# Encoder block on one core: eight instead of five of eleven down pairs by seven products, weight sums made ahead and kept in memory, one ring for weights, MLP chunks by pairs

## The chip, the cores and the metric

The kernel runs on one core of one Trainium2 chip. The metric is the device time of one execution in microseconds (us). Before the change, three runs gave 1457.05 to 1457.96 us, median 1457.39. The engines are named as in the profile: PE (matrix products), PEld (its loads of the stationary operand), DVE (vector engine), ACT (scalar engine), POOL, and SP, whose queue starts the loads.

## The reference, cut to what matters

```
x: (256, 2048) f32; D_FF = 5632
h = rms_norm(x); proj = h @ w_in                      # (2048, 10240)
ya = windowed_gqa(...); yb = dilated_attention(...)
x = x + (sigmoid(ga) * (ya @ w_branch_a) + sigmoid(gb) * (yb @ w_branch_b)) @ w_out
hf = rms_norm(x)
g = depthwise_conv3(hf @ w_ffn_gate) + conv_b
x = x + (gelu(g) * (hf @ w_ffn_up)) @ w_ffn_down      # the MLP: the change is mostly here
x = x + sigmoid(rms_norm(x) @ w_ple_gate) * (p @ w_ple_proj)
return rms_norm(x)
```

All data is f32. The gelu is computed by its tanh form.

## The kernel before, in words

**Precision.** A weight w is used as two parts: hi, which ACT rounds from w (L264), and lo = w - hi, which DVE makes (L265). Activations have two parts too. A product is hi times hi, plus the two cross terms. Where activations are the moving operand (`unit_blocks`, stages A and E) one block of 128 weight columns takes a matmul of 512 columns (L308) and one of 256 (L315). Where weights move (`thirds`, L365 to L367, stages B, D, F, pp, G) a product of 128 tokens, 128 inputs and 512 outputs takes three matmuls of 512 columns.

**Weights.** The host lays all weights out as pieces of 1 MB (128 x 2048 f32) in the order of use. SP loads one piece at a time into a ring of three buffers (`raw`). `produce` converts it by units of 1024 or 512 columns. The results go to rings of six units (`uh`, `ul`) and, for sums of weights, two more (`vh`, `vl`). A unit is converted as soon as `drop` has freed a place, so ACT and DVE run ahead of PE by at most the rings.

**Stages.** A: input projection and attention. B0 to B3: the gates, with the branch projections. D0, D1: output projection. Then the MLP in two halves of 22 chunks of 128 of the 5632 features: E0 makes the activations of a half (gate and up products of each chunk, 16 blocks each, then the convolution, gelu and product in `mlp`), F00 and F01 multiply them by the down weights, each for 1024 of 2048 output columns; then E1, F10, F11. pp and G end the block: projection of p, gate, final norm.

**Seven products for eight.** A stage of quads goes through its weights in pieces of two input chunks (a pair, 256 inputs) by two groups of 512 columns: four quarters. With two token halves, a plain piece (`s`) takes 8 products, 24 matmuls. A piece marked `S` takes 7 products (a Strassen-like scheme): four use sums of quarters of the weights and sums of the activations (`sums_of`). It has seven quarters to convert (3.5 units of 1024 columns) where a plain piece has four (two units), and DVE makes the weight sums in place (L257 to L259) in the stage itself. The table for the down stages is `DOWN = "SsSsSsSsSss"`: five of eleven pairs. `row_sums` puts the seven results together at the end of a stage.

**MLP chunks.** `mlp` handles one chunk of gate or up at a time, on tiles of 256 tokens: for gate, two reads of the product, the norm's factor, the convolution's three taps, then gelu; for up, factor, product with gelu, and the two parts for F (`halves`). The jobs go g0, g1, u0, g2, u1, ...

**End.** After the last stage each token half's last 512 columns are finished by columns of 256; then the sum of squares (L1109 to L1112), a power on POOL (L1114), the scaled rows (L1121) and the stores.

**Order.** PE, ACT, DVE and SP each have one queue in program order. The order on an engine is set when the kernel is built: by the program, within which a scheduler lets ready work go ahead of waiting work. Loads wait on the SP queue until their buffer is free.

## Time and profile before

| | |
|---|---|
| three runs | 1457.05, 1457.39, 1457.96 us |
| the profiled execution | 1457.96 us, of which the span is 1456.2 us |
| mean granted TensorE clock | 0.998 |
| PE, DVE, ACT busy | 99%, 86%, 56% of the span |
| read from and written to HBM | 279.49 and 2.14 MB |
| E0 | about 638.7 to 875 us of the span |
| F00, F01 | 875 to 988 |
| E1 | 988 to 1233 |
| F10, F11 | 1233 to 1349 |

"Busy" is time in which an instruction of the engine was under way. Matmuls overlap: each is recorded with its whole duration, and the next begins before it ends. So the time that one costs is the distance between starts. The same holds, to a lesser degree, for DVE and ACT.

### The profile page before, as it was taken

The numbers are of one execution on the slowest core, as the hardware profiler recorded it, in microseconds if no ns is written. First come the engines' busy times: TensorE is split into PE (matmuls) and PEld (weight loads), VectorE is DVE, ScalarE is ACT, GpSimd is POOL, SyncE is SP. The second block draws the span as 40 slices with busy tenths as digits, with TensorE's granted clock in tenths as the row PEclk, the third lists the DMA queues.
The fourth block names the chain that finished last, engine by engine and source line by source line (L and its number), as shares of the span: only waits on it lengthen the run. The fifth ranks groups of instructions, "written<-read, shape, count | busy, mean of one in ns | idle before, by whom it ended". The sixth has DMA issues, their size and how long they took to land.

```text
span 1456.2 us, 19520 instructions
## 1 busy us (share of the span) xinstructions
PE 1444.5 (99%) x7488; PEld 1235.9 (85%) x7488; DVE 1248.8 (86%) x1849; ACT 822.1 (56%) x1141; POOL 4.1 (0%) x9
## 2 busy tenths in 40 slices
PE   9999999999999999999999999999999999999997
PEld 8888888888888888888888888888888888888785
DVE  7677665679998989989888899989888889999995
ACT  7455544446555656666555555455555555565762
POOL 0000000000000000000000000000000000000000
PEclk9999999999999999999999999999999999999999
DMA  9654444535546456465554545565555554546462
GB/s 335 249 206 146 152 168 175 175 141 203 192 187 235 180 213 234 174 232 193 186 199 175 202 152 221 176 254 183 199 184 193 185 192 173 193 191 234 170 237 81
DMA packets 46312, 282.88 MB, mean 194 GB/s; under 512 B 4932, under 2 KB 9668, under 8 KB 13964
## 3 DMA queue, kind: packets, MB, share of 16 engines
q1 hardware_dynamic: 45500, 280.46, 53.2%
q8 instruction: 58, 0.95, 0.3%
q10 hardware_dynamic: 720, 1.19, 0.2%
q14 instruction: 34, 0.28, 0.1%
HBM read 279.49 MB, written 2.14 MB: 193 GB/s over the span
## 4 chain that ended last, share of the span: by engine, by line
PE 97%; DVE 1%; ACT 1%; issue 1%; DMA 0%; SPq 0%; POOL 0%; POOLq 0%; DVEq 0%; ACTq 0%
PE bank L308 29%; PE bank L315 15%; PE bank L365 14%; PE bank L366 14%; PE bank L367 14%; PE bank L354 2%; PE bank L356 2%; PE bank L355 2%; PE bank L292 1%; PE bank L293 1%; PE bank L870 1%; PE bank L687 0%; PE bank L635 0%; PE bank L634 0%; PE bank L633 0%
## 5 line engine op out<-in xcount | busy, mean ns | idle before, releaser
L264 ACT ACTIVATE uh<-raw 128x1024 fp32r<-128x1024 f32 (+2 forms) x518 | 522.3, 1017 | 399.5 <-PE bank L308 183.6
L265 DVE TENSOR_TENSOR ul<-raw,uh 128x1024 fp32r<-128x1024 f32 (+2 forms) x518 | 596.8, 1169 | 128.9 <-ACT uh L264 68.8
L308 PE MATMUL bank<-hf,uh 128*128 128x512 f32 x1408 | 336.3, 391 | 0.0
L308 PEld LDWEIGHTS bank<-hf,uh 128*128 128x128 f32 x1408 | 258.9, 188 | 50.2
L315 PEld LDWEIGHTS bank<-hf,ul 128*128 128x128 f32 x1408 | 180.4, 191 | 6.7
L315 PE MATMUL bank<-hf,ul 128*128 128x256 f32 x1408 | 182.8, 283 | 0.0
L264 ACT ACTIVATE vh<-raw 128x1024 fp32r<-128x1024 f32 x92 | 97.4, 1058 | 57.0 <-DVE raw L257 25.4
L265 DVE TENSOR_TENSOR vl<-raw,vh 128x1024 fp32r<-128x1024 f32 x92 | 111.9, 1219 | 0.4
L308 PE MATMUL bank<-hs,uh 128*128 128x512 f32 x432 | 103.6, 392 | 0.0
L456 ACT ACTIVATE t<-bank 128x256 f32<-128x256 f32 x122 | 46.5, 384 | 96.6 <-PE bank L315 89.5
L308 PEld LDWEIGHTS bank<-hs,uh 128*128 128x128 f32 x432 | 79.5, 188 | 15.6
L365 PE MATMUL bank<-uh,act 128*128 128x512 f32 x232 | 90.4, 390 | 0.0
L366 PE MATMUL bank<-ul,act 128*128 128x512 f32 x232 | 90.4, 390 | 0.0
L367 PE MATMUL bank<-uh,act 128*128 128x512 f32 x232 | 90.3, 389 | 0.0
L365 PE MATMUL bank<-uh,hs 128*128 128x512 f32 x172 | 67.3, 391 | 0.0
L367 PE MATMUL bank<-uh,hs 128*128 128x512 f32 x172 | 67.3, 391 | 0.0
L366 PE MATMUL bank<-ul,hs 128*128 128x512 f32 x172 | 67.1, 390 | 0.0
L257 DVE TENSOR_TENSOR raw<-raw 128x1024 f32<-128x1024 f32 x46 | 56.1, 1221 | 0.6
L315 PE MATMUL bank<-hs,ul 128*128 128x256 f32 x432 | 56.6, 284 | 0.0
L315 PEld LDWEIGHTS bank<-hs,ul 128*128 128x128 f32 x432 | 54.5, 191 | 1.0
L366 PE MATMUL bank<-vl,S 128*128 128x512 f32 x138 | 54.1, 392 | 0.1
L365 PE MATMUL bank<-vh,S 128*128 128x512 f32 x138 | 54.1, 398 | 0.0
(240 smaller groups left out, 2273.2 us busy)
## 6 DMA issues: line engine op xcount, KB each, us to landing
raw<-in_wts SPq DMA_DIRECT2D x251, 1024.0 KB, 4.8
raw<-in_wts SPq DMA_DIRECT2D x12, 512.0 KB, 7.2
xr<-in_xrow SPq DMA_DIRECT2D x4, 512.0 KB, 8.3
x<-in_xt SPq DMA_DIRECT2D x13, 128.0 KB, 6.0
hb<-hold SPq DMA_DIRECT2D x3, 514.0 KB, 5.9
hb<-hold SPq DMA_DIRECT2D x2, 768.0 KB, 7.5
last<-in_gainrow SPq DMA_DIRECT2D x1, 1024.0 KB, 6.9
out<-xr SPq DMA_DIRECT2D x4, 256.0 KB, 2.6
```

Source lines behind the costliest of these rows:

```text
L257: nc.vector.tensor_tensor(raw[:, :2 * WIDE], raw[:, WIDE:3 * WIDE], raw[:, :2 * WIDE], op=ALU.subtract)
L264: nc.scalar.activation(hi, src, AF.Copy)
L265: nc.vector.tensor_tensor(lo, src, hi.bitcast(F32), op=ALU.subtract)
L308: nc.tensor.matmul(acc, weights(u)[0][:, o * P:(o + 1) * P], m, start=first, stop=False, skip_group_check=True)
L315: nc.tensor.matmul(acc[:, T:], weights(u)[1][:, o * P:(o + 1) * P], m[:, :T], start=False, stop=last, skip_group_check=True)
L354: nc.tensor.matmul(acc[:, :n * P], xh, hi, start=(k == 0), stop=False)
L355: nc.tensor.matmul(acc[:, :n * P], xh, lo, start=False, stop=False)
L356: nc.tensor.matmul(acc[:, :n * P], xl, hi, start=False, stop=(k == KC - 1))
L365: nc.tensor.matmul(acc, sh, wh, start=first, stop=False, skip_group_check=True)
L366: nc.tensor.matmul(acc, sh, wl, start=False, stop=False, skip_group_check=True)
L367: nc.tensor.matmul(acc, sl, wh, start=False, stop=last, skip_group_check=True)
L456: keep(nc.scalar.activation(t, acc[:, T:], AF.Copy, scale=scale))
```

## The change

It has six parts.

1. **More pieces by seven products.** The down table becomes `ZZsZSZsZSZs`: eight of eleven pairs by seven products in each of the four F stages.
2. **Sums kept in memory.** Six of the eight are of a new kind `Z`. During E0 and E1 both halves of such a piece are loaded once more, DVE makes its four sums in place (`keep_sums`), and SP stores them to a buffer in HBM (`store_sums`). `_SUMS_AT` puts twelve of these into each half, after the 6th piece of the half and after every third from there. In F, a `Z` piece loads two quarters from the weights and four sums from that buffer, and needs no DVE sums. Every `S` piece, in the other stages too, now makes its sums into two tiles of their own, with four operations on 512 columns (L302 to L305) in place of one on 1024 and two on 512.
3. **One ring.** Raw weights and low parts share a ring of 12 tiles of 128 x 1024 (`SPLIT`); high parts have a ring of 7 (`ROUND`). Loads are of a unit (512 KB or 256 KB) and run at least four ahead of the conversion (`AHEAD`). The loads of the start are asked for step by step (`EARLY`).
4. **Pairs of chunks.** `mlp` reads each product at once but does the rest for two chunks together on tiles of 2 x 256; the middle tap moves to ACT, and a constant of the gelu into ACT's scale. An up chunk comes two gate chunks behind (`LAG`).
5. **The last products.** The last six matmuls of 512 columns are no longer cut into twelve of 256.
6. **The end.** On DVE the sum's last step (L1206) is kept ahead of the product with the gains (L1209).

PE's matmuls: 7452 - 6 = 7446 in place of 7488: 36 fewer in F, six fewer at the end.

```
-DOWN = "SsSsSsSsSss"
+DOWN = "ZZsZSZsZSZs"
...
     jobs = []
-    for f in range(FHALF + 1):
+    for f in range(FHALF + LAG):
         if f < FHALF:
             jobs.append(("g", half * FHALF + f))
-        if f:
-            jobs.append(("u", half * FHALF + f - 1))
+        if f >= LAG:
+            jobs.append(("u", half * FHALF + f - LAG))
...
+    for half in range(2):
+        ahead("E%d" % half, ("F%d0" % half, "F%d1" % half), 5, 3)
...
-        elif kind == "S":
-            cuts = [("n", 0, WIDE), ("n", 2 * WIDE, 4 * WIDE), ("T13", 0, 2 * WIDE), ("T24", 2 * WIDE, 4 * WIDE)]
+        elif kind in "SZ":
+            cuts = [("n", 0, WIDE), (kind + "13", 0, 2 * WIDE), (kind + "24", 2 * WIDE, 4 * WIDE),
+                    ("n", 2 * WIDE, 4 * WIDE)]
...
-RINGS = {"u": 6, "v": 2}
+SPLIT, ROUND = 12, 7
+AHEAD = 4
...
+    def keep_sums(p):
+        a, b = (raws[p, i] for i in range(2))
+        q = [w[:, i * WIDE:(i + 1) * WIDE] for w in (a, b) for i in range(2)]
+        nc.vector.tensor_tensor(q[1], q[1], q[0], op=ALU.subtract)
+        nc.vector.tensor_tensor(q[2], q[2], q[1], op=ALU.subtract)
+        nc.vector.tensor_tensor(q[3], q[3], q[2], op=ALU.subtract)
+        nc.vector.tensor_tensor(q[0], q[2], q[0], op=ALU.subtract)
+
+    def store_sums(p):
+        sums_in[p] = dram.tile([P, 4 * WIDE], F32, name="sums%d" % p)
+        for half in range(2):
+            cs = slice(2 * half * WIDE, 2 * (half + 1) * WIDE)
+            nc.sync.dma_start(sums_in[p][:, cs], raws.pop((p, half)))
...
+        while state["load"] < min(_LOAD_OF[last] + 1 + AHEAD, len(_LOADS)):
+            load()
+        if u == us[0]:
+            for q in _SUMS_AT.get(p - 1, ()):
+                keep_sums(q)
+            if _PIECES[p][0] == "S":
+                sums_of_weights(p)
+        if u == us[1]:
+            for q in _SUMS_AT.get(p - 1, ()):
+                store_sums(q)
+        n = b - a
+        w = raws.pop(u)[:, :n]
+        hi = wpool.tile([P, 2 * WIDE], FR, name="h", bufs=ROUND)[:, :n]
+        lo = wpool.tile([P, 2 * WIDE], FR, name="l", tag="w", bufs=SPLIT)[:, :n]
...
+            nc.vector.tensor_tensor(g, g, both(rt[1]), op=ALU.mult)
+            for i in range(2):
+                f = n - 1 + i
+                nc.scalar.activation(c[:, i], g[:, i], AF.Identity, scale=tap(1, f), bias=tap(3, f))
...
+            nc.scalar.activation(g, c, AF.Square, scale=math.sqrt(0.044715))
+            nc.vector.scalar_tensor_tensor(g, g, 1.0, c, op0=ALU.add, op1=ALU.mult)
+            nc.scalar.activation(g, g, AF.Tanh, scale=GELU_C)
+            nc.vector.scalar_tensor_tensor(c, g, 1.0, c, op0=ALU.add, op1=ALU.mult)
```

On DVE in E0, one gate chunk before, with the beginning of its up chunk (`u`, `gw`, `pair` are the chunk's tiles, `ul` low parts of weights):

```order
L460 TENSOR_TENSOR u<-bank,t 128x256
L981 TENSOR_TENSOR u<-u,rms 128x256
L982 TENSOR_SCALAR gw<-u,cl 128x256
L983 SCALAR_TENSOR_TENSOR gw<-u,cl,gw 128x255
L984 SCALAR_TENSOR_TENSOR gw<-u,cl,gw 128x255
L265 TENSOR_TENSOR ul<-raw,uh 128x1024
L986 TENSOR_SCALAR gw<-gw 128x256
L265 TENSOR_TENSOR ul<-raw,uh 128x1024
L987 TENSOR_TENSOR gw<-gw 128x256
L460 TENSOR_TENSOR pair<-bank,t 128x256
L995 SCALAR_TENSOR_TENSOR pair<-pair,rms 128x256
L996 TENSOR_TENSOR pair<-pair,gw 128x256
```

The same engine and half now, from the second gate chunk of a pair to the first of the four sums of a `Z` piece (`l` low parts, `w` raw weights):

```order
L527 TENSOR_TENSOR gw<-bank,t 128x256
L1061 TENSOR_TENSOR gw<-gw,rms 128x512
L344 TENSOR_TENSOR l<-w,h 128x1024
L1065 SCALAR_TENSOR_TENSOR gw<-gw,cl 128x255 x2
L1067 SCALAR_TENSOR_TENSOR gw<-gw,cl 128x255 x2
L344 TENSOR_TENSOR l<-w,h 128x1024
L1070 SCALAR_TENSOR_TENSOR gw<-gw 128x512
L344 TENSOR_TENSOR l<-w,h 128x1024
L1072 SCALAR_TENSOR_TENSOR gw<-gw 128x512
L344 TENSOR_TENSOR l<-w,h 128x1024
L527 TENSOR_TENSOR pair<-bank,t 128x256
L311 TENSOR_TENSOR w<-w 128x512
```

The middle tap and two of the gelu's steps are gone from DVE, most others are twice as wide and half as many, conversions stand between those that wait for ACT, and sums of weights have come into the half.

On DVE in F00, an `S` piece before:

```order
L257 TENSOR_TENSOR raw<-raw 128x1024
L258 TENSOR_TENSOR raw<-raw 128x512
L259 TENSOR_TENSOR raw<-raw 128x512
L265 TENSOR_TENSOR vl<-raw,vh 128x1024
L265 TENSOR_TENSOR ul<-raw,uh 128x1024
L265 TENSOR_TENSOR vl<-raw,vh 128x1024
L265 TENSOR_TENSOR ul<-raw,uh 128x1024
L265 TENSOR_TENSOR ul<-raw,uh 128x512
```

The same engine and stage now, with pieces `Z`, `s`, `Z` in the first three rows and then an `S` with its sums:

```order
L344 TENSOR_TENSOR l<-w,h 128x512
L344 TENSOR_TENSOR l<-w,h 128x1024 x5
L344 TENSOR_TENSOR l<-w,h 128x512
L344 TENSOR_TENSOR l<-w,h 128x1024 x3
L302 TENSOR_TENSOR w<-w 128x512
L304 TENSOR_TENSOR w<-w 128x512
L303 TENSOR_TENSOR w<-w 128x512
L344 TENSOR_TENSOR l<-w,h 128x512
L305 TENSOR_TENSOR w<-w 128x512
L344 TENSOR_TENSOR l<-w,h 128x1024 x3
```

Most pieces now have conversions alone there; two of eleven still have sums.

On DVE at the end, for the second token half, before (`known` and `v` are the sum of squares and the mean from it, `r` what POOL makes of `v`):

```order
L1108 TENSOR_TENSOR xr<-xr,c 128x256 x2
L1109 SCALAR_TENSOR_TENSOR c,ssq_12437<-xr 128x256 x2
L1111 TENSOR_TENSOR known<-known,ssq_12437 128x1
L1115 TENSOR_TENSOR xr<-xr,last 128x512
L1112 TENSOR_SCALAR v_13074<-ssq_12437,known 128x1
L1121 TENSOR_SCALAR xr<-xr,r_13077 128x512 x3
```

And now:

```order
L1202 TENSOR_TENSOR xr<-xr,c 128x256 x2
L1203 SCALAR_TENSOR_TENSOR c,ssq_13175<-xr 128x256 x2
L1205 TENSOR_TENSOR known<-known,ssq_13175 128x1
L1206 TENSOR_SCALAR v_13835<-ssq_13175,known 128x1
L1209 TENSOR_TENSOR xr<-xr,last 128x512
L1215 TENSOR_SCALAR xr<-xr,r_13838 128x512 x3
```

The product with the gains has moved behind the step that POOL waits for.

More of the change, by code (lines that the diff above doesn't have):

```diff
@@ L160, with _sums_at, ahead @@
 _PIECES, _STAGES = _pieces()
+def _sums_at():
+    at = {}
+    def ahead(hosts, stages, first, step):
+        pieces = [p for stage in stages for p in _STAGES[stage] if _PIECES[p][0] == "Z"]
+        for i, p in enumerate(pieces):
+            at.setdefault(_STAGES[hosts][first + i * step], []).append(p)
+    for half in range(2):
+        ahead("E%d" % half, ("F%d0" % half, "F%d1" % half), 5, 3)
+    return at
+_SUMS_AT = _sums_at()
 _NPIECES = len(_PIECES)
@@ L234, in _encoder @@
     sinks = cl[:, 3 * KC + 4 * FC:]
[L237 to L245 removed]
+    raws, made, sums_in = {}, {}, {}
+    state = {"load": 0, "unit": 0, "at": 0, "early": True, "free": ROUND}
@@ L283, in drop @@
         del made[u]
[L284 removed]
+        state["free"] += 1
         pump()
@@ L568, in _encoder @@
     ready = done = 0
-    for step in order:
+    for i, step in enumerate(order):
+        ask(i + EARLY)
         if len(step) == 3:
@@ L995, in mlp @@
[L995 to L1000 removed]
+            u = held["pair"]
+            gather(acc, u=u[:, k])
+            if k == 0:
+                return
+            nc.vector.scalar_tensor_tensor(u, u, 0.5, both(rt[1]), op0=ALU.mult, op1=ALU.mult)
@@ L1002, in _encoder @@
+            pair = m // 2
+            if DOWN[pair] != "s":
+                combos["act", pair] = sums_of(u, sum(c != "s" for c in DOWN[:pair]))
     ph_, pl_ = [], []
```

180 lines of the change are left out of this document (98 added, 82 removed).

## The prediction

> **What bounds the kernel now.** I read the page's totals first, then its chain, the waits, the stages one by one, and last the groups that the change touches.
>
> ```profile
> PE 1444.5 (99%) x7488; PEld 1235.9 (85%) x7488; DVE 1248.8 (86%) x1849; ACT 822.1 (56%) x1141; POOL 4.1 (0%) x9
> ...
> PE 97%; DVE 1%; ACT 1%; issue 1%; DMA 0%; SPq 0%; POOL 0%; POOLq 0%; DVEq 0%; ACTq 0%
> ```
>
> PE is busy nearly throughout and holds 97% of the chain that ended last. DVE comes next, with 86%. The waits say whether PE ever waits for the converted weights (here the longest of its waits for ACT's parts and for DVE's), and what the converters wait for:
>
> ```profile
> PEld bank L365 <- ACT vh L264: 1.1, 3, 0.4
> ...
> PEld bank L293 <- DVE ul L265: 1.0, 2, 0.7
> ```
> ```profile
> L265 DVE TENSOR_TENSOR ul<-raw,uh 128x1024 fp32r<-128x1024 f32 x468 | 563.8, 1220 | 115.8 <-ACT uh L264 56.5 <-PE bank L315 51.9 <-issue 6.2
> L264 ACT ACTIVATE uh<-raw 128x1024 fp32r<-128x1024 f32 x468 | 491.2, 1058 | 333.1 <-PE bank L308 178.3 <-PE bank L367 69.9 <-PE bank L356 40.8
> ```
>
> About 1 us in all for PE's loads, while both converters stand idle for PE: they have filled their rings and wait for a place. So PE sets the time and the converters have slack. Stage by stage, the columns being PE, PEld, DVE, ACT, POOL, clock, DMA share and GB/s (the start; then E0, both F of the first half):
>
> ```profile
> 0.00:30.00 30.00, 28.66 (x155) 24.91 (x156) 22.67 (x33) 24.30 (x37) 0.20 (x4) 1.00 0.93 329
> 660.00:860.00 200.00, 200.00 (x1152) 176.78 (x1151) 178.53 (x323) 111.82 (x169) 0.00 (x0) 1.00 0.54 190
> 875.00:988.00 113.00, 113.00 (x500) 93.43 (x500) 103.12 (x115) 60.76 (x67) 0.00 (x0) 1.00 0.57 210
> ```
>
> The clock is granted in full. In E0 DVE has 178.53 of 200 us (89.3%), in F 103.12 of 113 (91.3%), and DMA is at 54 to 57%.
>
> **The matmuls removed.** A matmul's price must not be read from its mean duration, since each begins before the last has ended:
>
> ```profile
> L365 PE MATMUL bank<-uh,act 128*128 128x512 f32 x232 | 90.4, 390 | 0.0
> ```
> ```profile
> 1439.80 0.39 PE L366 MATMUL bank<-ul,pl 128*128 128x512 f32 x1
> ...
> 1443.88 0.39 PE L366 MATMUL bank<-ul,pl 128*128 128x512 f32 x1
> ```
>
> Eighteen matmuls of 512 columns begin between 1439.80 and 1443.88: 4.08 / 18 = 0.227 us each. F's row agrees (113 / 498, two of its 500 being cut by the window's ends). Three more pairs by seven products save 3 x 3 matmuls in each of four stages, 36 x 0.227 = **8.2 us**. By the mean duration it would be 36 x 0.390 = 14.0 us, and 1443 in the end. The Trainium skill (Perfetto Trace Analysis, section Identifying the Most-Contended Engine) states that matmul busy time is no good measure since matmuls are pipelined. This trace agrees: 390 ns recorded, 227 ns spent. The last six products move the same columns uncut: nothing.
>
> **The end.** The last rows on DVE and POOL:
>
> ```profile
> 1448.90 0.15 DVE L1111 TENSOR_TENSOR known<-known,ssq 128x1 f32<-128x1 f32 x1
> 1449.01 0.69 DVE L1115 TENSOR_TENSOR xr<-xr,last 128x512 f32<-128x512 f32 x1
> 1449.62 0.21 DVE L1112 TENSOR_SCALAR v<-ssq,known 128x1 f32<-128x1 f32 x1
> 1449.91 0.55 POOL L1114 TENSOR_TENSOR r<-v,mhalf 128x1 f32<-128x1 f32 x1 [5.32 <-DVE v L1112]
> 1450.50 1.28 DVE L1121 TENSOR_SCALAR xr<-xr,r 128x512 f32<-128x512 f32 x3 [0.67 <-POOL r L1114]
> ```
>
> The product with the gains (L1115) holds up L1112 by 0.6 us while POOL waits. In the new order L1112 can start at about 1449.1, and the product runs beside POOL's 0.55. That is **-0.5 us** on the path, for all before it is serial after the last matmul.
>
> **DVE in the MLP halves.** The prices, from the groups of 44 us of E0, of 53 us of F01, and of the whole run:
>
> ```profile
> L265 DVE TENSOR_TENSOR ul<-raw,uh 128x1024 fp32r<-128x1024 f32 x16 | 19.3, 1221 | 4.6 <-PE bank L315 4.6
> L984 DVE SCALAR_TENSOR_TENSOR gw<-u,cl,gw 128x255 f32<-128x255 f32 x4 | 1.9, 485 | 0.1
> ...
> L982 DVE TENSOR_SCALAR gw<-u,cl 128x256 f32<-128x256 f32 x4 | 1.6, 412 | 0.1
> L986 DVE TENSOR_SCALAR gw<-gw 128x256 f32<-128x256 f32 x4 | 1.1, 286 | 0.0
> L853 DVE TENSOR_TENSOR S<-cmb,S 128x512 fp32r<-128x512 f32 x1 | 0.7, 685 | 0.0
> L850 DVE TENSOR_TENSOR cmb<-pair,cmb 128x128 f32<-128x128 f32 x1 | 0.3, 294 | 0.0
> ```
> ```profile
> L257 DVE TENSOR_TENSOR raw<-raw 128x1024 f32<-128x1024 f32 x4 | 4.9, 1220 | 0.1
> L259 DVE TENSOR_TENSOR raw<-raw 128x512 f32<-128x512 f32 x4 | 2.8, 688 | 0.1
> ```
> ```profile
> L852 ACT ACTIVATE S<-cmb 128x512 fp32r<-128x512 f32 x22 | 13.8, 629 | 8.8 <-DVE cmb L850 8.3
> ```
>
> A half is 22 gate and 22 up chunks of 16 blocks; E0's row has 1152 matmuls, 576 blocks, in 200 us, so a half is 704 x 0.347 = 244.4 us and DVE works 0.893 of it, 218.2 us. Gathers and conversions stay. Removed for a pair of chunks: for each chunk seven operations on 256 columns (0.412), two taps (0.485) and one constant (0.286), so 2 x 4.14 = 8.3 us. Added: six on 512 (0.688) and four taps, 6.1 us. Eleven pairs give -24 us. Added to the half: twelve times four sums on 512, 12 x 2.75 = 33 us, and three more sums of activations, 3 x (4 x 0.294 + 0.685) = 5.6 us. Together some +14: 232 of 244.4 us, **95%**, 1.1 us free in each 22.2 us (a pair's 64 blocks). So I cost all this work at nothing: PE's own 22.2 us hide it. If the cover went, the whole excess would be paid, as a rival below. ACT, at 111.82 of 200 us, has room for the middle tap and a wider square.
>
> **DVE in F.** An `S` piece costs sums of 1.22 + 2 x 0.688 = 2.6 and conversions of 0.69 (512 columns, as the sums) + 3 x 1.22 = 4.35 us, a plain one 2.44. Before: 5 x 6.95 + 6 x 2.44 = 49.4 us a stage. After: 8 x 4.35 + 2 x 2.75 + 3 x 2.44 = 47.6 us. The stage is 249 x 0.227 = 56.5 us before and 240 x 0.227 = 54.5 after, so DVE goes from 91.3% (51.6 us) to 49.8 / 54.5 = 91.4%: no change, and PE had no wait at that load. In B, D and G an `S` piece's sums go from 2.6 to 2.75 us: nothing where DVE waits for PE.
>
> **Loads, stores and the ring.** Bytes rise: a `Z` piece loads seven quarters in F, 1.835 MB for 21 x 0.227 = 4.77 us of PE; the stage is 6 x 1.835 + 5 x 1.049 = 16.3 MB in 54.5 us, 298 GB/s. In a half of E 44 pieces, twelve raw pieces again and their stores are 46.1 + 25.2 = 71.3 MB in 244.4 us, 292 GB/s. The rows scale to 329 / 0.93 = 354 GB/s at the start, where loads are mostly 512 KB or less, and 190 / 0.54 = 352 in E0. So both need some 83% of what these rows would give: enough on average, not with much to spare. The times to landing:
>
> ```profile
> raw<-in_wts SPq DMA_DIRECT2D x251, 1024.0 KB, 4.8
> raw<-in_wts SPq DMA_DIRECT2D x12, 512.0 KB, 7.2
> ...
> raw<-in_wts SPq DMA_DIRECT2D x2, 256.0 KB, 4.0
> ```
>
> A load is asked for when four units lie ahead of the conversion, and conversions run up to seven ahead of PE: eleven units, at 4.77 / 4 = 1.19 us each 13 us in F. Against it stand 7.2 us to land in the worst case shown and 2.3 us to convert. In E a unit is eight blocks, 2.8 us, and the lead 11 x 2.8 = 31 us. SP's queue is in order: each store waits for DVE's sums, and behind it the next weight loads. Before, its loads already waited so without harm:
>
> ```profile
> SPq L244 <- DVE ul L265: 754.9, 161, 11.8
> ```
>
> With 31 us of lead, a wait of up to that 11.8 us in E reaches nobody. No store is made in F. Bounds for the new ring: at best it removes a few of the start's stalls (28.66 of 30 us busy there, so under 1.4 us), at worst it lets loads of `Z` pieces come late. I take nothing, since the lead is longer than the worst landing shown.
>
> **Sum.** 8.2 + 0.5 = 8.7 us. The profiled execution took 1457.96 us with a span of 1456.2; it becomes 1449.3. The median of the runs lies 0.57 below it: 1457.39 - 8.7 = **1448.7 us**.
>
> **Rivals.**
>
> *Late loads in F.* The table begins with two `Z` pieces, 3.67 MB. At the 329 GB/s shown that takes 11.2 us against PE's 9.5: 1.6 us behind in each of four stages if the lead is already lost, 6.5 in all, and 1455. For it: DMA needs 83%. Against: plain and `S` pieces need 1.05 MB for 5.4 and 4.8 us and refill the lead. Most of its outcomes lie between 1450.5 and 1455.
>
> *DVE becomes the bound in E (slower).* Place: the pair's chain, where DVE waits for ACT's square and tanh, now 512 wide (0.629 each by L852's row), with the sums waiting for their loads in the same queue. Only 1.1 us in 22.2 are free. If DVE stood through both and through the middle taps, some 2.1 us a pair, 1.0 us would be paid 22 times: +22, and 1471. It decides from 1.1 us a pair. Against: the order has conversions between the waiting steps, and pairs halve the number of waits.
>
> *Half-size loads run one at a time (slower).* An F stage has 6 x 4 + 5 x 2 = 34 loads; at 4.0 us each and no overlap 136 us against 54.5, over 300 us slower in all. It decides when fewer than 34 x 4.0 / 54.5 = 2.5 are in flight. Against: the start moved 329 GB/s by such loads, far more than one in 4 us. The Trainium skill (DMA: Bandwidth & Descriptors, section Rules for kernel authors) asks for at least 1 MiB per DMA; the start's row speaks against its binding here.
>
> *PE is not the path.* The saved time turns up as other waits and the time stays at 1457. The chain's 97% speaks against it; that the matmuls are gone is plain from the order's count.
>
> **How the numbers follow.** The forecast has 0.62, late loads 0.18 (two thirds still faster by over 0.2%, a third within), DVE in E 0.14, half-size loads 0.03, no gain 0.03. A measurement of this kernel can tell about 0.2%, 2.9 us, from no change. So faster 0.62 + 0.12 = 0.74, same 0.06 + 0.03 = 0.09, slower 0.14 + 0.03 = 0.17. Low end: the sum with the start's 1.4 us, 1447.3, taken as 1447.0. High end: late loads with both bounds, 1455 and 2 us for what the rows don't show, 1457.0; above it lie the slower cases' 0.17 and the edge of "no gain".
>
> **What would show it.** Right: PE at 99% still, 240 matmuls in an F stage at 0.227 us, E0 still at 0.347 us a block with DVE near 95%, DMA near 0.83 in E and F, L1206 ahead of L1209. Wrong: PE waiting in E for `l` (DVE the bound), or in F for `h` or `l` whose conversion waited for a load; a start longer than before.

## The result, and the profile after

The changed kernel took 1498.36 us (median; 1498.18 to 1501.93), the kernel before beside it 1457.68 us: a ratio of 1.0283, with a 95% interval from 1.0266 to 1.0301. It is 41 us slower where 9 us faster were forecast. The profiled execution took 1498.48 us with a span of 1496.6.

The totals of the changed kernel's page:

```profile
PE 1451.1 (97%) x7446; PEld 1235.8 (83%) x7446; DVE 1256.6 (84%) x1781; ACT 843.0 (56%) x1153; POOL 5.0 (0%) x9
```

The matmuls are gone as counted, and PE is still busy for 97% of the span, but it waits. (The chain that ended last could be followed back over only some 15% of the span here, so it says little.) To see how much it waits, take for each two successive matmuls the time from start to start less the pitch of the first (0.227 us with 512 columns, 0.120 with 256, 0.1085 with 128). The pitches add up to 1431.6 us before and 1423.4 now: the 8.2 us of the forecast. The rest, PE's **excess**, went from 13.1 to 62.1 us. After the last product the span goes on for 9.9 us instead of 10.3. So -8.2 + 49.0 - 0.4 = 40.4 us, the whole difference of the spans (1496.6 - 1456.2).

The excess rose by 4.6 us in the first 100 us, 7.7 between 550 and 700 us (D), 13.7 from 700 to 1050 (E0's passage into F00 above all) and 23.4 beyond; from 100 to 550 it fell by 0.5.

The changed kernel's stretches (columns as in the prediction; E0, F, and the stretch behind PE's longest wait), and waits of the converters and of SP's queue over the whole run (us in total, times, longest):

```profile
660.00:860.00 200.00, 199.97 (x1150) 176.61 (x1149) 172.47 (x266) 105.83 (x152) 0.00 (x0) 1.00 0.87 292
...
895.00:1000.00 105.00, 103.16 (x447) 85.04 (x448) 93.70 (x107) 66.45 (x76) 0.00 (x0) 0.97 0.83 282
...
896.80:900.80 4.00, 3.96 (x9) 2.94 (x10) 3.45 (x5) 2.59 (x4) 0.00 (x0) 0.50 0.78 261
```
```profile
ACT h L343 <- DMA w<-in_wts: 144.4, 104, 5.3
...
SPq L292 <- DMA sums<-w: 71.8, 24, 5.0
SPq L321 <- DVE w L314: 41.1, 15, 5.4
```

ACT stands 144 us for weight loads (40.4 before). On SP's queue weight loads stand 72 us for stores of sums, whose tiles they need, and the stores stand for DVE's sums, with the weight loads queued behind. One of DVE's four groups of the sums in the 200 us of E0 (together 8.2 + 8.2 + 7.5 + 7.5 = 31.4 us):

```profile
L313 DVE TENSOR_TENSOR w<-w 128x512 f32<-128x512 f32 x12 | 8.2, 685 | 0.1
```

DVE isn't full in E0 (86%), but it is behind: with 31.4 us of sums it is only 12.9 us busier than in the kernel without them (159.54, below), so 18.5 us of other work is still to come at 860 us. At the end of E0 PE waits 7.3 us for the last gather (L527, which adds up the parts of a product), and that stands in DVE's queue behind the work left over. The rest of the wait's price is the clock, granted at 0.50 in the last of the stretches: L441, L442 and L443 then start 0.43 us apart instead of 0.227:

```profile
896.84 0.80 PE L441 MATMUL bank<-h,act 128*128 128x512 f32 x1 [7.26 <-DVE pair L527]
897.43 0.63 PE L442 MATMUL bank<-l,act 128*128 128x512 f32 x1
897.86 0.63 PE L443 MATMUL bank<-h,act 128*128 128x512 f32 x1
```

The best gauge is the **lead**: the time from the end of a low part's conversion to PE's first use of it. Its mean by the time of use, worked out from the starts and ends of L344 (L265 before) and of the matmuls; the last three columns are experiments below:

| from, us | before | changed | no sums in E | bytes in order | tiles held long |
|---|---|---|---|---|---|
| 680 | 13.4 | 11.2 | 16.5 | 15.5 | 11.2 |
| 720 | 14.1 | 9.7 | 16.7 | 15.5 | 10.0 |
| 760 | 14.1 | 7.4 | 16.6 | 14.4 | 5.7 |
| 800 | 14.1 | 3.5 | 16.8 | 14.8 | 3.3 |
| 840 | 12.7 | 2.5 | 16.6 | 14.2 | 3.3 |

Before, it stood at 13 to 14 us through E0; now it drains to 2.5 us, and again in E1 (12.6 us at 1040, 2.3 at 1160).

### The profile page after: what moved, and what is told of

Read it like the earlier page. It is cut to its first block, busy times and chain, and to the rows that moved or that the text cites. A ratio compares the mean times of both kernels' runs of the same rounds, so it can differ in the third digit from the quotient of the medians.

```text
span 1496.6 us, 20629 instructions
## 1 busy us (share of the span) xinstructions
PE 1451.1 (97%) x7446; PEld 1235.8 (83%) x7446; DVE 1256.6 (84%) x1781; ACT 843.0 (56%) x1153; POOL 5.0 (0%) x9
## 5 line engine op out<-in xcount | busy, mean ns | idle before, releaser
L343 ACT ACTIVATE h<-w 128x1024 fp32r<-128x1024 f32 (+2 forms) x634 | 628.0, 1013 | 436.0 <-DMA w<-in_wts 144.4
L344 DVE TENSOR_TENSOR l<-w,h 128x1024 fp32r<-128x1024 f32 (+2 forms) x634 | 727.2, 1166 | 83.8 <-ACT h L343 41.0
L384 PE MATMUL bank<-hf,h 128*128 128x512 f32 x1408 | 337.6, 391 | 3.4 <-ACT h L343 2.5
L384 PEld LDWEIGHTS bank<-hf,h 128*128 128x128 f32 x1408 | 258.5, 188 | 55.3 <-ACT h L343 3.8
L391 PEld LDWEIGHTS bank<-hf,l 128*128 128x128 f32 x1408 | 180.9, 191 | 15.0 <-DVE l L344 8.1
L391 PE MATMUL bank<-hf,l 128*128 128x256 f32 x1408 | 184.8, 283 | 6.3 <-DVE l L344 6.2
L384 PE MATMUL bank<-hs,h 128*128 128x512 f32 x432 | 103.6, 392 | 0.0
L441 PE MATMUL bank<-h,S 128*128 128x512 f32 x232 | 91.1, 403 | 5.4 <-DVE pair L527 3.6
L442 PE MATMUL bank<-l,S 128*128 128x512 f32 x232 | 92.0, 397 | 0.0
L443 PE MATMUL bank<-h,S 128*128 128x512 f32 x232 | 91.5, 395 | 0.0
L441 PE MATMUL bank<-h,act 128*128 128x512 f32 x192 | 74.3, 395 | 9.7 <-DVE pair L527 9.7
L442 PE MATMUL bank<-l,act 128*128 128x512 f32 x192 | 75.6, 395 | 1.1 <-DVE l L344 1.1
L443 PE MATMUL bank<-h,act 128*128 128x512 f32 x192 | 75.7, 395 | 0.0
L441 PE MATMUL bank<-h,hs 128*128 128x512 f32 x186 | 72.7, 391 | 0.0
L443 PE MATMUL bank<-h,hs 128*128 128x512 f32 x186 | 72.7, 391 | 0.0
L442 PE MATMUL bank<-l,hs 128*128 128x512 f32 x186 | 72.7, 391 | 0.0
L523 ACT ACTIVATE t<-bank 128x256 f32<-128x256 f32 x122 | 44.8, 370 | 41.3 <-PE bank L391 38.8
L441 PEld LDWEIGHTS bank<-h,S 128*128 128x128 f32 x232 | 44.7, 193 | 18.7 <-ACT h L343 5.2
L442 PEld LDWEIGHTS bank<-l,S 128*128 128x128 f32 x232 | 44.7, 193 | 9.1
```

The costliest lines, as they stand in the source:

```text
L343: nc.scalar.activation(hi, w, AF.Copy)
L344: nc.vector.tensor_tensor(lo, w, hi.bitcast(F32), op=ALU.subtract)
L384: nc.tensor.matmul(acc, weights(u)[0][:, o * P:(o + 1) * P], m, start=first, stop=False, skip_group_check=True)
L391: nc.tensor.matmul(acc[:, T:], weights(u)[1][:, o * P:(o + 1) * P], m[:, :T], start=False, stop=last, skip_group_check=True)
L441: nc.tensor.matmul(acc, sh, wh, start=first, stop=False)
L442: nc.tensor.matmul(acc, sh, wl, start=False, stop=False)
```

## The experiments

Each edit is against the changed kernel unless it says otherwise. Times are medians, with the ratio to the kernel before in the same runs and its 95% interval.

**What the kept sums cost.** Theory: their traffic in E makes the weight loads late. First rival: the one ring. Second: DVE's sums.

```
-DOWN = "ZZsZSZsZSZs"
+DOWN = "SsSsSsSsSss"
```

> The changed kernel with five down pairs of eleven by seven products again, all with sums made in F, as before; nothing is loaded, summed or stored for them in the MLP halves. The ring, the pairs of chunks, the order at the start and at the end stay as changed. Theory (the loads and stores of the kept sums make E's weight loads late): PE's excess over its pitches fell by 40 us in the stages from E0 to F11 and by some 15 us at the start, in D and in G, where no kept sum is under way. So this kernel has the matmuls of before, loses the 15 us and wins them nowhere: 1466 to 1474, with the lead of the converters over PE flat in E at about 14 us. First rival (the one ring of tiles is at fault in E as well): the lead drains in E here too, and the time is 1490 or more. Second rival (D's and the start's losses are only consequences of chance in one trace): 1458.

1471.66 us (1.0097, 1.0082 to 1.0112). The lead is flat (16.4 to 16.8 us from 680 to 860) and PE has no wait in E from 660 us on.

```
-        ahead("E%d" % half, ("F%d0" % half, "F%d1" % half), 5, 3)
+        ahead("E%d" % half, (), 5, 3)
...
-                src = sums_in[p]
+                src = wts[p]
```

> The changed kernel without anything of the kept sums in the MLP halves: no extra load, no subtraction on VectorE, no store. Left out are those sums themselves: the down stages read as many bytes from the unchanged weights in their place, with the same matmuls. Theory (traffic or work of the sums in E): the 34 us and more that PE lost from E0 to F11 go, and the time is 1460 to 1467, PE's waits in D and at the start stay. Rival (the ring, or the pairs of chunks, drain the lead by themselves): at most 10 us come back, 1488 or more.

1470.86 us (1.0093, 1.0078 to 1.0108): the kept sums cost **27.5 us**. Its E0:

```profile
660.00:860.00 200.00, 200.00 (x1152) 176.80 (x1151) 159.54 (x241) 120.49 (x167) 0.00 (x0) 1.00 0.60 188
```

It should have been 8.2 us under the run before it, by its 36 matmuls fewer, and is 0.8: its excess is 33.6 us against 27.3, and where F ends and after it PE waits for DVE's residual rows (`xr`) and for rows turned by PE and split by DVE (`pl`) (kernel without sums, some of PE's waits):

```profile
PE bank L441 <- DVE pl L540: 2.1, 1, 2.1
...
PE bank L384 <- DVE xr L1011: 1.5, 1, 1.5
PE bank L442 <- DVE l L344: 1.1, 1, 1.1
```

With five pairs the waits for `pl` are 1.1 us in all, where they are 2.9 here, and the other two are not there. So F, which PE now runs faster, is closed by DVE.

**Which part of the kept sums.** Copies in place of sums:

```
     def keep_sums(p):
...
-        nc.vector.tensor_tensor(q[1], q[1], q[0], op=ALU.subtract)
-        nc.vector.tensor_tensor(q[2], q[2], q[1], op=ALU.subtract)
-        nc.vector.tensor_tensor(q[3], q[3], q[2], op=ALU.subtract)
-        nc.vector.tensor_tensor(q[0], q[2], q[0], op=ALU.subtract)
```

> The changed kernel with the extra loads and the stores in the MLP halves, but without VectorE's four subtractions a pair: what is stored are copies of the weights, not their sums. Theory (the bytes on the DMA queues make the weight loads late): VectorE had idle time in E (172 us busy of 200), so little comes back: 1492 to 1499, and ScalarE's conversions wait for loads as before (some 140 us). Rival (VectorE's subtractions, 4 x 0.59 us and more a pair in bursts, hold up the low parts): 1460 to 1467.

1490.26 us (1.0222, 1.0198 to 1.0245), 8.1 us better and still 19 us over the kernel without sums. Stores issued by ACT instead of SP:

```
-            nc.sync.dma_start(sums_in[p][:, cs], raws.pop((p, half)))
+            nc.scalar.dma_start(sums_in[p][:, cs], raws.pop((p, half)))
```

> The changed kernel with the stores of the sums issued by ScalarE instead of SyncE; the bytes stay. In the changed kernel SyncE stood 62 us in all ahead of a store, waiting for VectorE's subtractions, with the next weight loads queued behind it. Theory (bytes, or the tiles held): 1494 to 1500. Rival (SyncE's order: loads late because a store ahead of them waits): the lead drains less, and 20 us or more come back, 1478 or less; ScalarE may lose some of it, since it waits in its turn.

1511.69 us (1.0374, 1.0357 to 1.0391), 13 us worse. That gives no support to SP's order as the cause, though ACT stands for the store in its turn. The Trainium skill (DMA: Bandwidth & Descriptors, section Rules for kernel authors) states that spreading DMAs over issuing engines doesn't help bandwidth; this run agrees: 285 GB/s in E0, against 292. Nor do the tiles come free sooner: SP's weight loads wait up to 8.4 us for a store, against 5.0.

Every second kept sum:

```
-        for i, p in enumerate(pieces):
-            at.setdefault(_STAGES[hosts][first + i * step], []).append(p)
+        for i, p in enumerate(pieces[::2]):
+            at.setdefault(_STAGES[hosts][first + i * 2 * step], []).append(p)
...
-                src = sums_in[p]
+                src = sums_in.get(p, wts[p])
```

> The changed kernel with every second kept sum only: six pairs an MLP half are loaded, summed and stored instead of twelve, one on every sixth piece of E instead of every third. The down stages keep their matmuls and bytes; for the other six pairs they read the unchanged weights, so that those pairs' sums are left out. E's demand falls from (3 x 1.049 + 2.097) MB in 16.7 us, 315 GB/s, to (6 x 1.049 + 2.097) MB in 33.4 us, 251 GB/s, where the changed kernel was served 282 to 292. Theory with a threshold (lead is lost only while more is asked than comes): nearly all of the 27.5 us that the kernel without sums won comes back, 1471 to 1477, with a lead in E that stays over 8 us. Rival (each kept sum costs its own 1.1 us, by a blocked queue or engine): half comes back, 1482 to 1487.

1470.64 us (1.0090, 1.0073 to 1.0106): half the sums cost nothing. There is a threshold, as the theory wanted. What it is a threshold of is asked by the next runs. The bytes without the tiles, by copies from memory to memory that GpSimd issues, with the kept loads and `keep_sums` taken out and two calls of `store_sums`:

```
-        loads += [(None, q, half) for q in _SUMS_AT.get(p, ()) for half in range(2)]
...
-            nc.sync.dma_start(sums_in[p][:, cs], raws.pop((p, half)))
+            nc.gpsimd.dma_start(sums_in[p][:, cs], wts[p][:, cs])
```

> The changed kernel without kept sums in the ring, on SyncE and on VectorE, but with their bytes: at the places where a piece's sums were stored, GpSimd issues two copies of the same 1.05 MB each from memory to memory, so the DMA engines move what the load and the store moved. Left out are the sums themselves; the down stages read the unchanged weights. Theory (the bytes on the DMA engines): close to the kernel with copies only, 1484 to 1494, and the lead drains in E. Rival (two tiles of the ring held from load to store, or the order on SyncE's queue): as without sums, 1470 to 1475, lead flat.

1553.53 us, inconclusive: the copies depend on nothing, so they went out from 1.2 us on and crowded the start, where the excess was 91 us in 200. The tiles without the bytes, `keep_sums` taken out:

```
-            a, b, src = 2 * half * WIDE, 2 * (half + 1) * WIDE, wts[p]
+            a, b, src = 0, 64, wts[p]
...
-            nc.sync.dma_start(sums_in[p][:, cs], raws.pop((p, half)))
+            nc.sync.dma_start(sums_in[p][:, cs][:, :64], raws.pop((p, half))[:, :64])
```

> The changed kernel with the kept sums' tiles of the ring, their loads and stores on SyncE at the same places, but only 64 of each tile's 1024 columns are loaded and stored, and VectorE's subtractions are left out: so the sums are left out, and the down stages read the unchanged weights. Theory (bytes): 1470 to 1474, as without sums, lead flat. Rival (two of the ring's twelve tiles held from load to store starve the weight loads): the lead drains as with copies, 1482 to 1492.

1473.46 us (1.0106, 1.0089 to 1.0123), lead flat. The copies issued by SP (against the kernel with GpSimd's):

```
-            nc.gpsimd.dma_start(sums_in[p][:, cs], wts[p][:, cs])
+            nc.sync.dma_start(sums_in[p][:, cs], wts[p][:, cs])
```

> As the kernel with the bytes elsewhere, but the two copies of 1.05 MB a piece, from memory to memory, are issued by SyncE, between the weight loads where the stores of the sums stood; with GpSimd they had all gone out ahead of time, most of them in the first 200 us, where the kernel lost 90 us. No tile is held and SyncE waits for nobody. Left out are the sums; the down stages read the unchanged weights. Theory (bytes): as with copies through tiles or worse, 1484 to 1510, the lead in E gone by the end of the half. Rival (tiles and order): 1470 to 1475.

1470.56 us (1.0086, 1.0071 to 1.0101), but the scheduler had moved the copies to between 51 and 376 us. So their order was held, and that of the loads:

```
-            nc.sync.dma_start(sums_in[p][:, cs], wts[p][:, cs])
+            tc.keep_in_program_order(nc.sync.dma_start(sums_in[p][:, cs], wts[p][:, cs]))
...
-        nc.sync.dma_start(t[:, :b - a], src[:, a:b])
+        part = nc.sync.dma_start(t[:, :b - a], src[:, a:b])
+        if not state["early"]:
+            tc.keep_in_program_order(part)
```

> As the kernel with the bytes in place, but SyncE's DMAs are held in the order in which they are written, so that the copies stand between E's weight loads: without that they had gone out between 51 and 376 us, where the DMA engines were 98% busy at 327 GB/s from 100 to 300 us and PE lost nothing. No tile is held for the copies. Left out are the sums; the down stages read the unchanged weights. Theory of before (the bytes are more than the DMA engines carry in E): 1484 to 1500, the lead in E gone by the end of the half. Rival, likelier now (the DMA engines had room at 0.87, and the bytes hurt because each waits in one of the ring's twelve tiles for its load, the subtraction and its store): 1470 to 1476, with a DMA share of 0.85 or more in E and the lead flat.

1470.87 us (1.0091, 1.0076 to 1.0106). Here the bytes do lie in E, as many as in the changed kernel and at a higher rate (its row, and its DMAs from 660 to 1000 us: count, size, median us to landing):

```profile
660.00:860.00 200.00, 200.00 (x1150) 176.67 (x1149) 158.58 (x236) 115.09 (x164) 0.00 (x0) 1.00 0.90 309
```
```profile
w<-in_wts SPq DMA_DIRECT2D x138, 512.0 KB, 6.0
sums<-in_wts SPq DMA_DIRECT2D x48, 512.0 KB, 8.2
```

309 GB/s, and PE waits for nothing. My theory of the bytes fell here. The tiles alone again, each store one piece later:

```
         if u == us[1]:
-            for q in _SUMS_AT.get(p - 1, ()):
+            for q in _SUMS_AT.get(p - 2, ()):
```

> The kernel with the kept sums' tiles only (64 of 1024 columns loaded and stored), with each store one piece later, so that each tile of the ring is held some 5.6 us longer, about as long as the full store took (5.8 us) beside the small one. Left out are the sums; the down stages read the unchanged weights. Theory of the held tiles: the lead in E drains without the bytes, 1478 to 1495. Theory of the bytes: as with the tiles only, 1470 to 1476.

1472.56 us (1.0104, 1.0088 to 1.0121), but it didn't do what I meant: the small store still went out 2.2 us after its load. From the issues of the 48 pairs on SP, a kept tile waits from load to store 14.0 us in the changed kernel, 5.4 with copies, 2.3 with tiles only; the store's landing adds 5.0, 4.3 and 1.5. With the loads and stores of that kernel held in order too, by the same calls as above:

> The kernel with the kept sums' tiles only, 64 of 1024 columns loaded and stored, with SyncE's DMAs held in written order and each store two pieces after the first possible place, so that eight weight loads stand between a tile's load and its store. In the run with the tiles held they had not been: a tile's store went out 2.2 us after its load (in the changed kernel 14.0 us, plus 5.0 us until the store has landed; with copies only 5.4 and 4.3 us). Here it is about 20 us. Left out are the sums; the down stages read the unchanged weights. Theory of the held tiles (two of the twelve, some 19 us each, and two more every 16.7 us or less): the lead in E drains without the bytes, 1480 to 1500. Rival (bytes and tiles only hurt together, since a weight load then needs longer and so more tiles): 1470 to 1478.

1476.03 us (1.0136, 1.0108 to 1.0163; its profiled execution is the slowest of four, 1484.39). Tiles held for 20.8 us, with no bytes to speak of, and in this execution E0 looks as in the changed kernel: the lead drains in the same steps (table above), ACT waits as long for weight loads, and PE waits 4.7 us for DVE's last gather on the way into F. Its E0 row, and ACT's wait there, in the 200 us where the changed kernel's ACT waited 53.9 us:

```profile
660.00:860.00 200.00, 199.94 (x1147) 176.41 (x1146) 148.42 (x222) 107.19 (x155) 0.00 (x0) 1.00 0.57 185
```
```profile
ACT h L334 <- DMA w<-in_wts: 58.1, 35, 6.1
```

Loads come late at a DMA share of 0.57, so here they wait for **tiles of the ring**, not for DMA time. By Little's rule (tiles in use are tiles taken per us, times the us for which each is held) two tiles for 14.0 + 5.0 = 19 us in every 16.7 us are 2.3 of the twelve, where PE's lead of low parts takes six or seven.

But a drained lead isn't yet the time. The median is only 5 us above the kernel without sums, outside the theory's range and inside the rival's, that bytes and tiles only hurt together; and the trace is of an execution 8 us slower than that median. What the runs show is this. The bytes alone cost nothing; the tiles alone, 2.7 of them, 5 us in the median; with copies, where tiles are held for 9.7 us (1.2 tiles) and 291 GB/s flow, 19 us. With half the sums 1.1 tiles (11.8 + 6.3 us in every 33.4) cost nothing at 251 GB/s. Why both together cost more than their sum stays open. That loads land later (6.1 us with copies, 5.0 with half the sums) isn't enough by itself: with the bytes in order they took 8.0 us in E0, and nothing was lost. A rival that no run excludes is the order on SP's queue. In the run with copies the stores stand there for the loads of their own tiles:

```profile
SPq L317 <- DMA w<-in_wts: 38.8, 19, 6.5
```

That is 38.8 of E0's 200 us, with weight loads queued behind: the store at 690.3 us had stood for 6.5 us, and the two weight loads behind it went out within 1 us, waiting for nothing. In the changed kernel the stores stand 30.4 us for DVE's sums, with half the sums 5.5, and in the two runs with the bytes alone and the tiles held long not at all. Stores on ACT don't settle it, since ACT, which converts the weights, then stands for them (2.2 us at 743.7, for one).

**The start.** On the kernel with five pairs, low parts and input rows kept in the order in which they are written:

```
-        nc.vector.tensor_tensor(lo, w, hi.bitcast(F32), op=ALU.subtract)
+        low = nc.vector.tensor_tensor(lo, w, hi.bitcast(F32), op=ALU.subtract)
+        if state["early"]:
+            tc.keep_in_program_order(low)
...
-        nc.vector.scalar_tensor_tensor(dst[:, T:], src, g, dst[:, :T].bitcast(F32),
-                                       op0=ALU.mult, op1=ALU.subtract)
+        low = nc.vector.scalar_tensor_tensor(dst[:, T:], src, g, dst[:, :T].bitcast(F32),
+                                             op0=ALU.mult, op1=ALU.subtract)
+        if state["early"]:
+            tc.keep_in_program_order(low)
```

> The changed kernel with five down pairs by seven products (no kept sums), and VectorE's instructions of the first stretch held in the order in which they are written: the low parts of the first two weight units stand ahead of the second to fifth input rows again, as before the change. Theory (PE waits at the start because those low parts stand behind rows that have not come): the 3.4 us of the first 50 us come back, 1467.5 to 1469. Rival (at the start the loads or the ring are late, whatever the order): under 1 us, 1471 to 1472.5.

In the kernel with five pairs the first two low parts stood behind four input rows, and PE waited for them (PE's wait, and DVE's row; before the change they began at 5.33 us, behind one row):

```profile
PE bank L369 <- DVE l L344: 3.0, 1, 3.0
```
```profile
9.91 1.15 DVE L344 TENSOR_TENSOR l<-w,h 128x384 fp32r<-128x384 f32 x2
```

1472.90 us (1.0103, 1.0088 to 1.0118). That wait is gone, but one of 4.7 us has come, since the sum of squares now stood ahead of a low part (DVE's row, and PE's wait):

```profile
18.29 1.23 DVE L641 TENSOR_TENSOR squares<-squares,sq 128x1024 f32<-128x1024 f32 x1 [5.52 <-ACT sq L639]
```
```profile
PE bank L371 <- DVE l L344: 4.7, 1, 4.7
```

With that sum in the order as well:

```
-            nc.vector.tensor_tensor(squares, squares, q, op=ALU.add)
+            both = nc.vector.tensor_tensor(squares, squares, q, op=ALU.add)
+            if state["early"]:
+                tc.keep_in_program_order(both)
```

> As the kernel with the start in order, but the sum of the squares is held in that order too: there it had come ahead of a low part and VectorE stood 5.5 us for ScalarE's square, while PE waited 4.7 us. Theory (the start's loss is VectorE's order alone): PE's excess in the first 50 us falls from 7.9 us to 4.5 to 5, 1467.5 to 1469. Rival (the loads are late at the start, since low parts and loaded weights share twelve tiles): another wait appears, and 1470.5 or more stays.

1466.60 us (1.0059, 1.0044 to 1.0074): **5.1 us** back, and no wait of PE's between the first 1.1 us and D. The low parts are early again:

```profile
5.72 1.21 DVE L344 TENSOR_TENSOR l<-w,h 128x384 fp32r<-128x384 f32 x2
```

PE's excess in the first 100 us is 4.3 us, 5.1 before the change: the start's loss was DVE's order alone.

**D.** On the kernel with five pairs, a ring of six:

```
-SPLIT, ROUND = 12, 7
+SPLIT, ROUND = 12, 6
```

> The changed kernel with five down pairs by seven products (no kept sums) and a ring of six converted units instead of seven; nothing else differs. With seven, the converters led PE by 4.5 to 6 us in the B stages and at D's entry (before, with eight units in two rings: 7 to 8 us), and PE's excess over its pitches between 550 and 700 us was 11.2 us, of which 1.8 us before the change. Theory (D's loss is the shorter lead): with six units the lead at D's entry is 2 to 4 us, and D loses 5 to 15 us more: 1477 to 1490, with new waits in the B stages possible. Rival (D's loss is another, of the order of the cuts or the sums): D's excess unchanged within 1 us, 1470 to 1474.

1472.65 us (1.0103, 1.0088 to 1.0119); D's excess fell to 7.5 us instead of rising, against my theory. On the same kernel, the order of before within a pair by seven products:

```
-            cuts = [("n", 0, WIDE), (kind + "13", 0, 2 * WIDE), (kind + "24", 2 * WIDE, 4 * WIDE),
-                    ("n", 2 * WIDE, 4 * WIDE)]
+            cuts = [("n", 0, WIDE), ("n", 2 * WIDE, 4 * WIDE), (kind + "13", 0, 2 * WIDE),
+                    (kind + "24", 2 * WIDE, 4 * WIDE)]
...
-                sums_of_weights(p)
+            if u == us[2]:
+                sums_of_weights(p)
```

> The changed kernel with five down pairs by seven products (no kept sums), and the order of before within a pair by seven products: both plain units first, then the four sums and the two units of sums, with the products in the order of before; the four sums of weights come just ahead of the third unit instead of ahead of the first. The ring stays as changed. Theory now (D's loss is VectorE's order: in D0's end its first low part of hf came at 594.4 us before and at 602.6 us in the kernel with five pairs, with sums and conversions ahead of it): PE's excess between 550 and 700 us falls from 11.2 us to under 5, 1462 to 1467. Rival (the shared ring sets that order, whatever the cuts): unchanged within 2 us, 1470 to 1474.

1473.01 us (1.0101, 1.0086 to 1.0116); D's excess 10.2 us, as the rival said. On the kernel with the start in order, DVE's rows of D0 and D1 held in written order (sums of weights, low parts, `c`, residual rows):

```
+    def inorder(ins):
+        if state["early"] or state.get("D"):
+            tc.keep_in_program_order(ins)
...
-            nc.vector.tensor_tensor(r, r, a, op=ALU.add)
+            inorder(nc.vector.tensor_tensor(r, r, a, op=ALU.add))
```

> The kernel with the whole start in order (five down pairs by seven products, no kept sums), with VectorE's sums, low parts and residual rows of D0 and D1 held in the order in which they are written as well: the residual rows of D0 stand directly behind the stage's last sums again. Theory (D's loss is VectorE's order): PE's excess between 550 and 700 us falls from 11.1 us to 5 or less, 1459 to 1462. Rival (the ring of seven and twelve is too short for D, in any order): another wait appears in its place, 1465 to 1468.

1468.98 us (1.0079, 1.0064 to 1.0094), 2.4 us worse: other waits in the same place. Last, fewer pairs by seven products in D, on the kernel with the start in order:

```
-        quads("D%d" % s, ("w_out", 2 * s * WIDE), ("w_out", (2 * s + 1) * WIDE), ALT)
+        quads("D%d" % s, ("w_out", 2 * s * WIDE), ("w_out", (2 * s + 1) * WIDE), "Ssssssss")
```

> The kernel with the whole start in order (five down pairs by seven products, no kept sums), with one instead of four pairs by seven products in each of D0 and D1; the others by eight, 18 matmuls more, 4.1 us. Theory (D's loss comes from the pairs by seven products there: each takes eight of the ring's twelve tiles, where the ring of before made the sums in the loaded weights' own tile): PE's excess between 550 and 700 us falls from 11.1 us to 4 or less, 1461 to 1464. Rival (it comes from the end of D0 and D1 itself, residual rows and turns, whatever the pairs): excess 9 us or more, 1469 to 1472.

1460.95 us (1.0024, 1.0014 to 1.0033): 5.7 us less with 4.1 us more of matmuls, so **9.7 us** were D's. The longest of PE's waits in D in the kernel with the start in order, then D's rows in the kernel before and with plain pairs:

```profile
PE bank L443 <- DVE hf L542: 2.2, 1, 2.2
PE bank L443 <- ACT h L343: 1.8, 3, 1.0
```
```profile
560.00:660.00 100.00, 99.99 (x491) 83.18 (x490) 91.67 (x123) 61.95 (x85) 0.71 (x1) 1.00 0.62 221
```
```profile
560.00:660.00 100.00, 100.00 (x495) 84.00 (x494) 68.55 (x86) 52.49 (x71) 0.70 (x1) 1.00 0.62 209
```

The pairs by seven products in D cost it, in the changed kernel's ring. Whether by the tiles they take or by the DVE work (68.55 of 100 us here) stays open; in the kernel before, DVE carried the four pairs at 91.67 of 100 us without a wait of PE's.

**A version with all of it.** Start and D in order, and:

```
-DOWN = "SsSsSsSsSss"
+DOWN = "ZSsZSsZSsZs"
...
-        ahead("E%d" % half, ("F%d0" % half, "F%d1" % half), 5, 3)
+        ahead("E%d" % half, ("F%d0" % half, "F%d1" % half), 3, 5)
```

> The kernel with the start and D in order, with seven of eleven down pairs by seven products: three with sums made in F and four with sums kept from E, so eight kept sums an MLP half, one on every fifth piece, instead of twelve on every third. It computes the whole reference. E's demand is (5 x 1.049 + 2.097) MB in 27.9 us, 263 GB/s, where 282 to 292 were served. 24 matmuls go against five pairs, 5.4 us. Theory (a threshold of the traffic in E; the rest is order): 5 us under the kernel with D in order, 1454 to 1458. Rival (each kept sum costs its own share, or F's VectorE cannot carry it): no gain, 1460 or more.

1477.95 us (1.0140, 1.0125 to 1.0155), 9 us worse than without kept sums, where 5 better were expected. E's lead holds at 11 to 14 us, so eight sums a half don't drain it; but against the kernel with D in order the excess grew by 6.7 us between 600 and 700 us, where D ends and the kept sums begin, by 2.7 between 700 and 1050, most of it where E1 begins, and by 4.9 between 1250 and 1400, where the second half's F stages end. No version here beats the kernel before.

## Why the prediction was wrong, point by point

*Matmuls removed, -8.2 us.* Right on PE's pitches (1431.6 to 1423.4). But "PE sets the time and the converters have slack" was wrong for the ends of F: with three more pairs in each F stage than the run with five, and no sums in E, 0.8 of the 8.2 us came through in the medians (1.9 between the profiled executions), since F's ends then wait for DVE. The prediction looked at F's load (91.4%; measured 93.70 of 105 us, 89.2%), not at what must follow F's last product.

*The end, -0.5 us.* Measured 9.9 against 10.3 us after the last product: right.

*DVE in the MLP halves, hidden.* The load was right: 172.47 of 200 us, and with the 18.5 left over 95.5%, where 95% was forecast. But "PE's own 22.2 us hide it" failed: the subtractions' part is 8.1 us. I hold the longer stay of the tiles in the ring (19 against 9.7 us) for its reason, with 1.1 us free in 22.2 too little for DVE to catch up once loads come late; no run separates this from DVE's time. The rival "DVE becomes the bound in E", with 1471, was the nearest on size, but DVE stood idle for 14% of E0, and without the subtractions 19 of the 27 us stay.

*Loads, stores and the ring, nothing.* Here it failed, at the sentence "With 31 us of lead, a wait of up to that 11.8 us in E reaches nobody". From the issue of a load to PE's first use of its low part it is indeed 30.8 us in E0 without the kept sums, and still 28 to 31 with their bytes alone. In the changed kernel it falls from 24 us at 680 us to 15 at 840, in the run with copies to 15, and in the trace of the tiles held long to 16. The eleven units counted the ring's twelve tiles as if all were for low parts and weight loads; two of them, for 19 us of every 16.7, belong to the kept sums, and their stores stand in the queue of the weight loads. The lead was taken as fixed, and the change itself used it up. The rate was right (292 GB/s, at a share of 0.87 where 0.83 was forecast), and so was "enough on average": the DMA engines carried 309 GB/s without harm. Price: 27.5 us, DVE's 8.1 among them. How the rest divides between tiles, slower loads and SP's order stays open, beyond the 5 us of the tiles alone.

*The new ring, "I take nothing, since the lead is longer than the worst landing shown".* With the order that came with it, it cost 5.1 us at the start, by DVE's order, and 9.7 us in D, where the lead of the low parts and not a landing was the measure.

Together 27.5 + 9.7 + 5.1 and 7.4 at F's ends (8.2 - 0.8) are 49.7 us, against 49.0 us of added excess. That they meet so closely is partly luck: the terms were measured on different kernels, and in the changed kernel's own trace the excess grew by 4.6 us at the start and by 7.7 in D.

*The rivals.* "Late loads in F" named the right wait in the wrong stage. "Half-size loads one at a time" is refuted by 309 GB/s in loads of 512 KB. "PE is not the path" had the chain's 97% against it, and that was read too far: a chain full of PE says that PE set the time at its old speed, and nothing of how far behind it the others stand. The lead would have: in D it was near 0.2 us for some low parts of sums in the kernel before as well.

## What to carry to other kernels

When new work borrows buffers from a ring, multiply the tiles it takes by the time from load to release and compare that with the ring, not only the bytes with the bandwidth. Ask also what stands behind its stores in an in-order queue: here bytes alone cost nothing, tiles alone little, and both together much. A lead that was worked out for the old use of a ring is not there for the new one. Count the lead of the producers over the bound engine, stage by stage, before removing work from that engine; in this kernel it was smallest at the ends of stages, and there the cut stopped paying. Where a scheduler sets an engine's order, read the order of the first instructions after any change: most of 5 us lay in two low parts behind four rows.

## What the runs showed of the hardware

A wait of PE can cost more than its length. In the changed kernel the clock stood at 0.50 for 3.4 or 6.8 us in five places (from 9.9, 894.0, 1269.5, 1348.0 and 1402.6 us), behind waits of 1.9, 7.4, 2.6 with 2.8, 1.0 with 1.2, and 2.4 us (from start to start of two matmuls, less the pitch), and 9.4 us of the excess are matmuls at the doubled pitch; before, none but behind the last product. The Trainium skill (TensorE: Matmul & The Clock Gate, part The HAM clock gate) gives windows of some 3.4 us and half rate after an idle one. The lengths agree; but here the clock also fell behind waits shorter than such a window, 2.39 us at 1399.9 us for one, and didn't behind one of 2.37 us at 613.3. This trace suggests a reason: the five falls lie on one grid of 3.413 us (259, 369, 392 and 408 steps after the first), and in the step that ends at each PE lost 1.92, 3.41, 2.61, 2.25 and 2.39 us. In no other step at full clock, before the last product, did it lose more than 1.83, since the wait at 613.3 lies across an edge of the grid at 614.1. In other runs steps with a loss of 1.75 to 2.2 us went either way.
